# A weighted sum of two experts' outputs: the first small write of zeroes is taken out

## The chip, the core and the metric

The kernel runs on one core of one Trainium2 chip. The metric is the device time of one execution in microseconds; of three runs of the kernel before, the median is 238.86 us (238.84 to 238.99). The profile is of one execution, taken by the hardware profiler.

## The reference

Each of 16 x 1024 = 16,384 tokens has two vectors of 512 float32 numbers, one from each of its two experts, and two weights. The output is the weighted sum.

```python
# expert_outputs (16, 1024, 2, 512) f32, combine_weights (16, 1024, 2) f32
def reference(expert_outputs, combine_weights):
    weights = combine_weights[..., np.newaxis]
    return np.sum(expert_outputs * weights, axis=2).astype(np.float32)
```

The inputs are 67.2 MB (4 KB a token) and the output 33.6 MB (2 KB a token).

## The kernel before

The tokens are laid out over the 128 partitions: each partition holds 128 of them (`per`), the first 115 (`main`) from one contiguous stretch of the tokens and the last 13 (`LAST`) from another. A token's place in its partition is called `t`.

*Buffers.* One large tile, `et`, has room for 51 tokens a partition, cut into four rooms of 13, 13, 12 and 13 (`ROOM`). A tile of work is the 12 or 13 tokens a partition that fill one room; ten such tiles (`TILES`) make up the 128, and tile g uses room g mod 4. The output of a tile is written over its input, in the first half of a room, and stored from there. `wt` holds all the weights, 256 numbers a partition. `zt`, 16 x 128 numbers, holds zeroes, and `warm` is one column.

*Loads.* All loads of the expert outputs are issued by SP (L76). The first tile comes in two parts, of 2 and of 11 tokens a partition, so there are five loads ahead of the loop (`FIRST`): 1024, 5632, 6656, 6144 and 6656 KB. The first of them is cut into pieces of 4 KB. The other six are issued in the loop, each when the store out of its room is done.

*Small DMAs at the start.* ACT issues four, in this order: the zeroes (L111), the weights of the first 115 tokens a partition (L79, 920 bytes a partition), and the weights of the last 13 in two halves of 64 partitions (L114). Then it runs one activation on a constant (L115), which brings its table load with it. The zeroes are made by a memset on VectorE (L108). They go to the output itself: its first 115 x 128 rows are seen as 16 long rows, and the first 128 numbers of each (512 bytes) are written with zeroes. The tiles' results are stored over them later.

*The loop.* It runs over nine stores (`STORES`); tiles 7 and 8 share one. For tiles 0 to 7 `combine` multiplies a whole tile by its weights in one VectorE operation (L88) and adds the two halves in another (L97). Tile 8 shares its first product with ScalarE (L92, L94, L96, then L97). Tile 9 goes token by token: ScalarE scales one expert's vector (L102), and VectorE multiplies the other one and adds (L103). ACT issues the first seven stores and SP the last two (L130). SP then issues the load of the tile that takes the room's place (L76).

*Order.* The order of instructions on each queue is that of the program; the framework adds the waits. DMAs signal through a small set of semaphores used in turn, so a DMA also waits until the one that had its semaphore before it has landed.

Of the kernel before, what the change touches and what calls it, by code (L numbers as in the profile page):

```python
# [1 line left out]

# [4 lines left out]


@with_exitstack
def kernel(  # L10
    ctx: ExitStack,
    tc: tile.TileContext,
    expert_outputs: bass.AP,
    combine_weights: bass.AP,
    out: bass.AP,
):

    nc = tc.nc
    b, s, k, h = expert_outputs.shape
    assert k == 2
    n = b * s
    P = nc.NUM_PARTITIONS
    per = n // P
    assert per * P == n

    ROOM = [13, 13, 12, 13]
    ROOMS = len(ROOM)  # L30
    SITE = [sum(ROOM[:i]) for i in range(ROOMS)]
    TILES = [13, 13, 12, 13, 13, 13, 12, 13, 13, 13]
    FIRST = [2, 11, 13, 12, 13]
    STORES = [[0], [1], [2], [3], [4], [5], [6], [7, 8], [9]]
    WHOLE = [0, 1, 2, 3, 4, 5, 6, 7]
    MIXED = [8]
    ALONE = 3
    FREE = {9: 0}
    LAST = 13
    assert all(c <= ROOM[g % ROOMS] for g, c in enumerate(TILES))  # L40
    assert sum(TILES) == per and [g for st in STORES for g in st] == list(range(len(TILES)))
    main = per - LAST
    starts = [sum(TILES[:g]) for g in range(len(TILES))]

    def rows(x):

        first = x[0 : P * main, :].rearrange("(p t) f -> p t f", p=P)
        second = x[P * main : n, :].rearrange("(p t) f -> p t f", p=P)
        return lambda t, c: first[:, t : t + c, :] if t < main else second[:, t - main : t - main + c, :]

    flat = out.rearrange("b s h -> (b s) h")
    eo = rows(expert_outputs.rearrange("b s k h -> (b s) (k h)"))
    cw = rows(combine_weights.rearrange("b s k -> (b s) k"))
    o = rows(flat)

    dt = mybir.dt.float32
    mult = mybir.AluOpType.mult
    add = mybir.AluOpType.add
    copy = mybir.ActivationFunctionType.Copy

    pool = ctx.enter_context(tc.tile_pool(name="all", bufs=1))
    et = pool.tile([P, sum(ROOM), k * h], dt)
    halves = et.rearrange("p j (k h) -> p (j k) h", k=k)
    wt = pool.tile([P, per * k], dt)
    wk = wt.rearrange("p (t k) -> p t k", k=k)
    zt = pool.tile([16, 128], dt)
    warm = pool.tile([P, 1], dt)

    def place(t):
        g = max(g for g in range(len(TILES)) if starts[g] <= t)  # L70
        return SITE[g % ROOMS] + t - starts[g]

    def load(t, c, **kw):
        at = place(t)
        assert place(t + c - 1) == at + c - 1
        nc.sync.dma_start(out=et[:, at : at + c], in_=eo(t, c), **kw)  # L76

    def weights(q, t, c):
        q.dma_start(out=wk[:, t : t + c, :], in_=cw(t, c))  # L79

    def combine(g, base):
        at, c, t0 = SITE[g % ROOMS], TILES[g], starts[g]
        if g in WHOLE or g in MIXED:
            room = halves[:, k * at : k * (at + c), :]
            x0, x1 = et[:, at : at + c, 0:h], et[:, at : at + c, h : 2 * h]
            if g in WHOLE:
                wb = wt[:, k * t0 : k * (t0 + c)].unsqueeze(2).to_broadcast([P, k * c, h])
                nc.vector.tensor_tensor(out=room, in0=room, in1=wb, op=mult)  # L88
            else:
                for i in range(ALONE, c):  # L90
                    x = et[:, at + i, 0:h]
                    nc.scalar.activation(out=x, in_=x, func=copy, scale=wt[:, k * (t0 + i) : k * (t0 + i) + 1])  # L92
                w1 = wk[:, t0 : t0 + c, 1:2].to_broadcast([P, c, h])
                nc.vector.tensor_tensor(out=x1, in0=x1, in1=w1, op=mult)  # L94
                w0 = wk[:, t0 : t0 + ALONE, 0:1].to_broadcast([P, ALONE, h])
                nc.vector.tensor_tensor(out=x0[:, 0:ALONE], in0=x0[:, 0:ALONE], in1=w0, op=mult)  # L96
            nc.vector.tensor_tensor(out=halves[:, base : base + c, :], in0=x0, in1=x1, op=add)  # L97
            return
        for i in range(c):
            t = k * (t0 + i)  # L100
            x0, x1 = halves[:, k * (at + i), :], halves[:, k * (at + i) + 1, :]
            nc.scalar.activation(out=x0, in_=x0, func=copy, scale=wt[:, t : t + 1])  # L102
            nc.vector.scalar_tensor_tensor(  # L103
                out=halves[:, base + i, :], in0=x1, scalar=wt[:, t + 1 : t + 2], in1=x0, op0=mult, op1=add
            )

    with tc.manual_schedule():
        nc.vector.memset(zt, 0.0)  # L108

        ahead = flat[0 : P * main, :].rearrange("(q t) h -> q (t h)", q=16)  # L110
        nc.scalar.dma_start(out=ahead[:, 0:128], in_=zt)  # L111
        weights(nc.scalar, 0, main)
        for half in (slice(0, P // 2), slice(P // 2, P)):
            nc.scalar.dma_start(out=wk[half, main:per, :], in_=cw(main, per - main)[half])  # L114
        nc.scalar.activation(out=warm, in_=nc.const_aps.tensor(1.0, (P, 1), dt), func=copy)  # L115

        t = 0
        for i, c in enumerate(FIRST):
            load(t, c, **({"max_dma_last_dim": k * h * 4} if i == 0 else {}))
            t += c  # L120
        assert t == sum(TILES[:ROOMS])
        for j, st in enumerate(STORES):
            room = FREE.get(st[0], st[0] % ROOMS)
            base, c = SITE[room] * k, 0
            for g in st:
                combine(g, base + c)
                c += TILES[g]
            assert c <= k * ROOM[room]
            q = nc.sync if j in (7, 8) else nc.scalar
            q.dma_start(out=o(starts[st[0]], c), in_=halves[:, base : base + c, :])  # L130
            for g in st:
                if g + ROOMS < len(TILES):
                    load(starts[g + ROOMS], TILES[g + ROOMS])


# [1 line left out]
_INS = ['expert_outputs', 'combine_weights']  # L137
_OUTS = [((16, 1024, 512), 'float32')]


# [23 lines left out]
```

## Time and profile before

| | |
|---|---|
| median of three runs | 238.86 us |
| profiled execution, first to last instruction (span) | 237.1 us |
| VectorE busy | 190.0 us (80%), 33 instructions |
| ScalarE busy | 15.8 us (7%) |
| moved | 100.80 MB in 3344 packets, 425 GB/s over the span |
| queue q1 (issued by SP) | 2000 packets, 77.33 MB |
| queue q10 (issued by ACT) | 1344 packets, 23.47 MB |
| of the zeroes: memset, issue, issue to landing | 0.17 us, 0.39 us, 3.9 us |

The page gives no time of its own for the profiled execution beyond its span; the median of the runs stands 1.8 us above that span. In the profile, "issue" rows of SPq and ACTq are the time in which a sequencer issues a DMA, not the transfer; the time from issue to landing is listed apart, and contains the wait behind other transfers. The DMA row gives the mean busy share of the core's 16 DMA engines in tenths. A name such as out_dram<-zt reads "written from zt to the output".

### The profile page before, as it was taken

What the parts mean: (1) busy time and instruction counts of PE and PEld (TensorE: products, weight loads), DVE (VectorE), ACT (ScalarE), POOL (GpSimd) and SP (SyncE); (2) the same over time, 40 slices, a digit from 0 to 9 for tenths busy, and PEclk for the clock granted to TensorE, in tenths of its full rate; (3) what the DMA queues carried; (4) which work ended last, traced back from release to release, by engine and by line L of the source; (5) the groups of instructions that cost most, each with busy time, mean ns of one, the idle gap of its engine ahead of it and who ended that gap; (6) DMA issues with size and microseconds to landing.
All of it is one profiled execution on the core that took longest, in us unless ns stands there. A gap on an engine that the chain in (4) does not pass through costs nothing.

```text
span 237.1 us, 154 instructions
## 1 busy us (share of the span) xinstructions
DVE 190.0 (80%) x33; ACT 15.8 (7%) x25; POOL 0.2 (0%) x4
## 2 busy tenths in 40 slices
DVE  0006999999999999999999998998499969919400
ACT  2000000000000000000000000000000055019200
POOL 0000000000000000000000000000000000000000
DMA  8999999989999999999899999999899999899996
GB/s 300 388 481 434 432 421 398 470 348 485 449 431 458 431 440 390 486 420 420 359 492 409 409 509 392 431 503 431 359 431 503 420 397 483 381 431 431 431 431 287
DMA packets 3344, 100.80 MB, mean 425 GB/s; under 512 B 512, under 2 KB 656, under 8 KB 912
## 3 DMA queue, kind: packets, MB, share of 16 engines
q1 hardware_dynamic: 2000, 77.33, 75.9%
q10 hardware_dynamic: 1344, 23.47, 23.0%
HBM read 67.24 MB, written 33.56 MB: 425 GB/s over the span
## 4 chain that ended last, share of the span: by engine, by line
DVE 55%; DMA 36%; issue 1%; ACT 0%; DVEq 0%; ACTq 0%; SPq 0%
DVE et L88 35%; DVE et L97 17%; DMA out_dram<-et 17%; DMA et<-in_expert_outputs_dram 12%; DMA wt<-in_combine_weights_dram 8%; DVE et L103 3%; ACT et L102 0%; DVEq L159 0%; ACTq L111 0%; DVE zt L108 0%; DVEq L88 0%; SPq L76 0%; ACTq L102 0%
## 5 line engine op out<-in xcount | busy, mean ns | idle before, releaser
L88 DVE TENSOR_TENSOR et<-et,wt 128x13312 f32<-128x13312 f32 (+1 forms) x8 | 110.0, 13754 | 23.8 <-DMA wt<-in_combine_weights_dram 18.7
L97 DVE TENSOR_TENSOR et<-et 128x6656 f32<-128x6656 f32 (+1 forms) x9 | 62.8, 6973 | 0.4
L92 ACT ACTIVATE et<-et,wt 128x512 f32<-128x512 f32 x10 | 6.2, 708 | 188.0 <-DMA et<-in_expert_outputs_dram 188.0
L103 DVE SCALAR_TENSOR_TENSOR et<-et,wt 128x512 f32<-128x512 f32 x13 | 8.7, 747 | 5.0 <-ACT et L102 5.0
L102 ACT ACTIVATE et<-et,wt 128x512 f32<-128x512 f32 x13 | 8.1, 707 | 14.0 <-DMA et<-in_expert_outputs_dram 14.0
L94 DVE TENSOR_TENSOR et<-et,wt 128x6656 f32<-128x6656 f32 x1 | 7.1, 7093 | 2.3 <-DMA et<-in_expert_outputs_dram 2.3
L96 DVE TENSOR_TENSOR et<-et,wt 128x1536 f32<-128x1536 f32 x1 | 1.8, 1751 | 0.0
L115 ACT ACT_TABLE_LOAD x1 | 1.3, 1283 | 3.1 <-issue 3.1
L108 DVE MEMSET zt<- 16x128 f32 x1 | 0.2, 165 | 0.8 <-PEq L148 0.8
L115 ACT ACTIVATE warm<-const-float32-1.0 128x1 f32<-128x1 f32 x1 | 0.2, 203 | 0.0
L148 POOL MEMSET const-bfloat16-1.0<- 128x1 bf16 x1 | 0.1, 102 | 0.0
L148 POOL MEMSET const-uint8-127<- 128x1 uint8 x1 | 0.1, 101 | 0.0
L148 POOL MEMSET const-float32-0.0<- 128x1 f32 x1 | 0.1, 99 | 0.2 <-issue 0.2
L148 POOL MEMSET const-float32-1.0<- 128x1 f32 x1 | 0.1, 98 | 0.0
## 6 DMA issues: line engine op xcount, KB each, us to landing
et<-in_expert_outputs_dram SPq DMA_DIRECT2D x7, 6656.0 KB, 32.2
out_dram<-et ACTq DMA_DIRECT2D x5, 3328.0 KB, 34.7
et<-in_expert_outputs_dram SPq DMA_DIRECT2D x2, 6144.0 KB, 41.1
out_dram<-et SPq DMA_DIRECT2D x1, 6656.0 KB, 19.9
out_dram<-et ACTq DMA_DIRECT2D x2, 3072.0 KB, 37.2
et<-in_expert_outputs_dram SPq DMA_DIRECT2D x1, 5632.0 KB, 18.2
out_dram<-et SPq DMA_DIRECT2D x1, 3328.0 KB, 14.0
et<-in_expert_outputs_dram SPq DMA_DIRECT2D x1, 1024.0 KB, 5.0
```

The lines of the kernel that those rows point to most:

```text
L88: nc.vector.tensor_tensor(out=room, in0=room, in1=wb, op=mult)
L92: nc.scalar.activation(out=x, in_=x, func=copy, scale=wt[:, k * (t0 + i) : k * (t0 + i) + 1])
L94: nc.vector.tensor_tensor(out=x1, in0=x1, in1=w1, op=mult)
L96: nc.vector.tensor_tensor(out=x0[:, 0:ALONE], in0=x0[:, 0:ALONE], in1=w0, op=mult)
L97: nc.vector.tensor_tensor(out=halves[:, base : base + c, :], in0=x0, in1=x1, op=add)
L102: nc.scalar.activation(out=x0, in_=x0, func=copy, scale=wt[:, t : t + 1])
L103: nc.vector.scalar_tensor_tensor(out=halves[:, base + i, :], in0=x1, scalar=wt[:, t + 1 : t + 2], in1=x0, op0=mult, op1=add)
L108: nc.vector.memset(zt, 0.0)
L115: nc.scalar.activation(out=warm, in_=nc.const_aps.tensor(1.0, (P, 1), dt), func=copy)
L148: nc = _bacc.Bacc("TRN2", target_bir_lowering=False, num_devices=1)
```

## The change

The tile `zt`, its memset on VectorE and the DMA that writes it to 16 rows of the output are removed. Nothing else is edited. ACT's first DMA is then that of the weights.

```diff
     wk = wt.rearrange("p (t k) -> p t k", k=k)
-    zt = pool.tile([16, 128], dt)
     warm = pool.tile([P, 1], dt)
...
     with tc.manual_schedule():
-        nc.vector.memset(zt, 0.0)
-
-        ahead = flat[0 : P * main, :].rearrange("(q t) h -> q (t h)", q=16)
-        nc.scalar.dma_start(out=ahead[:, 0:128], in_=zt)
         weights(nc.scalar, 0, main)
         for half in (slice(0, P // 2), slice(P // 2, P)):
             nc.scalar.dma_start(out=wk[half, main:per, :], in_=cw(main, per - main)[half])
```

## The prediction

> **What bounds the kernel now.** I read the page first: its busy shares, the row of the DMA engines in forty slices, and the bytes.
>
> ```profile
> span 237.1 us, 154 instructions
> DVE 190.0 (80%) x33; ACT 15.8 (7%) x25; POOL 0.2 (0%) x4
> DMA  8999999989999999999899999999899999899996
> DMA packets 3344, 100.80 MB, mean 425 GB/s; under 512 B 512, under 2 KB 656, under 8 KB 912
> ```
>
> VectorE is busy for 80% of the span, but the row of the DMA engines reads 8 or 9 in every slice but the last. To see whether a transfer ever has to wait for an instruction, I took stretches of the windows view: the time before the first packet, the first load, two stretches in the middle, and the time behind the last packet. The columns are start:end, length, busy time of DVE, ACT and POOL, the clock, the share of the DMA engines and GB/s.
>
> ```profile
> 0.00:1.80 1.80, 0.17 (x1) 0.00 (x0) 0.20 (x4) 1.00 0.00 0
> 1.80:5.00 3.20, 0.00 (x0) 1.49 (x2) 0.00 (x0) 1.00 0.99 315
> 5.00:18.60 13.60, 0.00 (x0) 0.00 (x0) 0.00 (x0) 1.00 1.01 435
> 75.00:100.00 25.00, 24.97 (x3) 0.00 (x0) 0.00 (x0) 1.00 1.00 431
> 235.66:237.10 1.44, 0.00 (x0) 0.00 (x0) 0.00 (x0) 1.00 0.01 0
> ```
>
> The span is nearly a ledger of DMA work. 100.80 MB at 433 GB/s, the middle of 431 and 435, are 232.8 us; 1.80 us pass before the first packet and 1.44 us behind the last; that is 236.0 of 237.1 us. The rest, 1.1 us, is lost where the engines are occupied but slow. The first such place is visible above: in 1.80 to 5.00 they are 99% occupied and move 315 GB/s. At 433 GB/s the same bytes take 3.20 x 315/433 = 2.33 us, so 0.87 us go there. I looked for a second place around the first output store, whose issue the timeline gives (start, length). The three stretches below it are of the DMA view, 36.2 to 43.4, 43.4 to 46.1 and 46.1 to 51.0 us. Queue q1 carries what SP issues, the loads; q10 what ACT issues; the columns are packets, MB and share of 16 engines.
>
> ```profile
> 40.91 0.34 ACTq L130 DMA_DIRECT2D out_dram<-et  x1
> ...
> q1 hardware_dynamic: 64, 3.15, 101.0%
> ...
> q1 hardware_dynamic: 16, 0.79, 81.6%
> q10 hardware_dynamic: 16, 0.43, 36.6%
> ...
> q1 hardware_dynamic: 32, 1.57, 75.0%
> ```
>
> All these q1 packets belong to one load of the same 49,152 bytes a packet. Before the store's first packets one takes 1.010 x 7.2 x 16 / 64 = 1.82 us; just as they begin, 0.816 x 2.7 x 16 / 16 = 2.20 us; after that 0.750 x 4.9 x 16 / 32 = 1.84 us. So each engine loses about 0.38 us once, at the first store. 0.87 and 0.38 us are 1.25 us, which closes the ledger to within the 0.2 us that the choice of rate leaves open.
>
> Last, whether VectorE's waits could move the end. From the chain of waits (start, length, what):
>
> ```profile
> 1.43 18.21 DMA wt<-in_combine_weights_dram
> ...
> 19.73 14.04 DVE et L88
> ...
> 144.62 39.25 DMA out_dram<-et
> ...
> 183.92 28.80 DMA et<-in_expert_outputs_dram
> ```
>
> From 144.62 us the chain runs through transfers. Up to there VectorE is on it, but transfers are never out of work meanwhile (431 GB/s in 75 to 100 us). What a change does to the time is therefore what it does to the DMA engines: bytes taken away, and time lost in which they stand or crawl.
>
> **The change part by part.** What goes and what stands around it, from the timeline and from the table of issues (KB, us from issue to landing):
>
> ```profile
> 0.73 0.44 SPq L76 DMA_DIRECT2D et<-in_expert_outputs_dram  x1
> 0.81 0.17 DVE L108 MEMSET zt<- 16x128 f32 x1 [0.81 <-PEq L148]
> 1.01 0.39 ACTq L111 DMA_DIRECT2D out_dram<-zt  x1
> 1.22 0.46 SPq L76 DMA_DIRECT2D et<-in_expert_outputs_dram  x1
> 1.43 0.45 ACTq L79 DMA_DIRECT2D wt<-in_combine_weights_dram  x1
> 1.91 1.16 ACTq L114 DMA_DIRECT2D wt<-in_combine_weights_dram  x2
> et<-in_expert_outputs_dram SPq DMA_DIRECT2D x1, 5632.0 KB, 18.2
> et<-in_expert_outputs_dram SPq DMA_DIRECT2D x1, 1024.0 KB, 5.0
> wt<-in_combine_weights_dram ACTq DMA_DIRECT2D x1, 115.0 KB, 18.2
> out_dram<-zt ACTq DMA_DIRECT2D x1, 8.0 KB, 3.9
> ```
>
> *The memset, 0.17 us*, is alone on VectorE, which has nothing to do before 19.73 us: nothing on the path. If VectorE started at once it would cost 0.17 us.
>
> *The zeros' packets.* In 4.0 to 4.6 us the DMA view has them, 16 packets of data and 16 that signal:
>
> ```profile
> q1 hardware_dynamic: 59, 0.24, 97.7%
> q10 hardware_dynamic: 32, 0.01, 6.0%
> ```
>
> 0.060 x 0.6 us = 0.036 us of each engine. By the ledger this is gained whole: -0.04 us.
>
> Against this row stands a rule. The Trainium skill, page "DMA: Bandwidth & Descriptors", section "Rules for kernel authors", says that a transfer under 64 KB is mostly overhead. By it the 3.9 us to landing of this 8 KB transfer would be nearly all overhead to be saved; the trace does not agree that it is on the path, since the loads kept 97.7% of the engines meanwhile.
>
> *The weights move up.* ACT waits for the memset until 1.01 us and issues the weights at 1.43. Without both it can issue them as soon as SP issues its first load, at 0.73 us, 0.70 us sooner, and the two tail DMAs behind them likewise. In 8 to 10 us the queues alternate, one packet of the weights (920 bytes) for one of the load of 5632 KB on each engine:
>
> ```profile
> q1 hardware_dynamic: 16, 0.72, 83.2%
> q10 hardware_dynamic: 16, 0.01, 2.1%
> ```
>
> So eight packets of weights took eight load packets of 0.832 x 2 = 1.66 us to get through, and landed at 1.43 + 18.21 = 19.64 us. If they come up among the small packets of the first load, they land before the 5632 KB load does, and then that load is next to be late: issued at 1.22, landed at 19.4 us. VectorE starts 0.2 to 0.3 us sooner. By the ledger this is worth nothing at the end; without the cover of saturated engines it would be worth those 0.3 us.
>
> *The two sequencers meet.* The issue that all else waits for, SP's first at 0.73, now meets ACT's long one in place of the zeros' at 1.01. An issue of SP beside one of ACT takes up to 0.64 us (least, median and most of the four in ns stand in the second row), one that is alone 0.33:
>
> ```profile
> 2.20 0.64 SPq L76 DMA_DIRECT2D et<-in_expert_outputs_dram  x1
> L76 SPq DMA_DIRECT2D et<-in_expert_outputs_dram x4: 424/449/643, 0.7 to 2.2; - x4
> 67.80 0.33 SPq L76 DMA_DIRECT2D et<-in_expert_outputs_dram  x1
> ```
>
> The first takes 0.44 now. At worst the weights' issue goes wholly ahead of it, +0.45 us; at best nothing. I take 0.64 - 0.44 = +0.20 us, since every delay before the first packet is added to the span. The Trainium skill, page "Perfetto Trace Analysis", section "DMA Instruction — HWDGE (DVE, Sync)", says that two sequencers share one block that generates descriptors; the longer issues agree, and no row here shows which comes first.
>
> *The first write.* The zeros are the first bytes that the kernel writes to the output, one small packet on each of 16 engines, at a time when a write can be held up without holding up the loads. Two first uses are seen to cost the engines time: 0.87 us at the first load, 0.38 us at the first store, and the second of these with the zeros long landed. If a first write has a cost of its own, the zeros paid it hidden, and the store at 40.91 us now pays it with full engines. The trace cannot show it. From below, it is zero: the zeros landed 3.9 us after issue with no dent in the loads. From above, it is the 0.87 us of the first load. A gain is excluded by the loads' 97.7% in those 0.6 us. I take the nearest row, the same event with large packets: +0.38 us, a stall that doubles.
>
> *The fifth load.* SP's queue shows one wait on the zeros:
>
> ```profile
> SPq L76 <- DMA out_dram<-zt: 2.1, 1, 2.1
> 4.92 0.33 SPq L76 DMA_DIRECT2D et<-in_expert_outputs_dram  x1
> et<-in_expert_outputs_dram SPq DMA_DIRECT2D x1, 6656.0 KB, 71.7
> et<-in_expert_outputs_dram SPq DMA_DIRECT2D x1, 6144.0 KB, 50.9
> ```
>
> The fifth load shares a semaphore with the zeros and is held until they have landed. It is issued at 4.92 us and lands 71.7 us later, behind the fourth load, which is issued at 2.20 and lands at 2.20 + 50.9 = 53.1 us. So it stood in the queue for some 48 us. Whether another DMA holds it next or none, its place in the queue is the same: 0. It would matter only if it were held until shortly before 53 us.
>
> Sum: -0.04 + 0.20 + 0.38 = +0.54 us. The profiled span of 237.1 becomes 237.6 us; the median of the runs, 238.86, stands 1.8 us above the span, outside the instructions, which the change leaves alone. So 238.86 + 0.54 = 239.4 us, 0.23% slower.
>
> **The rivals.**
>
> *Work is conserved, no change.* The two plus terms are zero; -0.04 us gives 238.8 us. For it: the ledger, and zeros that landed without a dent in the loads. Against it: both stalls that the ledger needs sit at a first use. Chance 0.36, and 0.02 more for a change that only moves the fifth load's wait.
>
> *Faster: a cleaner start.* The slow 3.2 us hold the issue of the zeros and of three weight DMAs among the first loads' issues. If the crowd of issues is what starves the first load, one issue fewer and the weights out of the way sooner give back part of the 0.87 us. At half, 0.44 + 0.04 = 0.48 us: 238.4 us. It decides from the point at which the start window's rate passes 365 GB/s (0.44 us less for the same bytes). Against it: packets are slowest at the very beginning, while the zeros' packets pass at full rate. Chance 0.13.
>
> *Faster by the whole wait.* If the fifth load's 2.1 us in SP's queue came through to the end: 238.86 - 2.1 = 236.8 us. That needs the queue of loads to run dry, and the load stood in it for some 48 us. It is also what the overhead rule above would make of the time. Chance 0.02.
>
> **How the numbers follow.** The forecast's case, a slower start or a slower first store, has 0.47. A measurement of this kernel can tell about 0.2%, 0.48 us, from no change; so the forecast lies just past that bound, with its own range from 238.9 to 240.2 (+0.45 and +0.87, less 0.04). The cases give faster 0.15, same 0.38, slower 0.47. The range over all reaches down to 238.3, which takes in the conserved case and the cleaner start at a little over half, and up to 240.2.
>
> **What would show it.** In the changed profile: ACT's first issue near 0.7 us and SP's first issue longer than 0.44; the first packet later than 1.8 us; the weights landing before the 5632 KB load, and VectorE starting near 19.5; above all the packets of the fourth load, 1.82 us each, stretching to more than 2.2 us when the first store begins. If they stretch as before and the first packet comes at 1.8, the conserved case is right and I am wrong. If the rate in the first 3.2 us of packets rises past 365 GB/s, it is the cleaner start.

## The result and the profile after

The changed kernel takes 239.69 us, the median of six runs, against 238.89 us for the kernel before: a ratio of 1.0026 with a 95% interval of 1.0016 to 1.0036. That is slower by 0.8 us in the medians, and inside the forecast range (239.4, 238.3 to 240.2).

The six runs are not one cluster. Five lie between 239.53 and 239.74 us and one at 238.85, where the kernel before stands. The profile after is of that one. A second profile, of a run at 239.55 us, is that of the run "same_again" below. I call the two the short and the long execution of the changed kernel. Of eleven runs in both series one is short.

The page of the short execution has the span and the busy times of the kernel before:

```profile
span 237.1 us, 151 instructions
DVE 189.9 (80%) x32; ACT 15.8 (7%) x25; POOL 0.2 (0%) x4
```

The long one spans 237.8 us. The timelines of both begin with the same two issues, short first, then long. ACT's weights and SP's first load are issued within 0.01 us of each other, where the kernel before had 0.28 us between SP's load and ACT's zeroes:

```profile
0.72 0.43 ACTq L78 DMA_DIRECT2D wt<-in_combine_weights_dram  x1
0.73 0.44 SPq L75 DMA_DIRECT2D et<-in_expert_outputs_dram  x1
...
0.72 0.45 ACTq L78 DMA_DIRECT2D wt<-in_combine_weights_dram  x1
0.73 0.42 SPq L75 DMA_DIRECT2D et<-in_expert_outputs_dram  x1
```

Where the long execution loses its 0.7 us is seen in four stretches of the windows view, in this order: the start, the first store, the whole middle, the tail. First the kernel before (its start stands in the prediction), then the long execution:

```profile
41.00:52.00 11.00, 11.00 (x1) 0.00 (x0) 0.00 (x0) 1.00 0.97 402
52.00:212.00 160.00, 148.90 (x17) 6.23 (x10) 0.00 (x0) 1.00 1.00 433
235.40:237.00 1.60, 0.00 (x0) 0.00 (x0) 0.00 (x0) 1.00 0.01 0
...
1.80:5.00 3.20, 0.00 (x0) 1.49 (x2) 0.00 (x0) 1.00 0.98 315
41.00:52.00 11.00, 11.00 (x2) 0.00 (x0) 0.00 (x0) 1.00 0.98 383
52.00:212.00 160.00, 149.26 (x17) 6.23 (x10) 0.00 (x0) 1.00 1.00 434
235.40:237.00 1.60, 0.00 (x0) 0.00 (x0) 0.00 (x0) 1.00 0.16 67
```

The start moves 315 GB/s in both and the 160 us of the middle 433 and 434. The 11 us around the first store drop from 402 to 383 GB/s, which is 11 x 19/402 = 0.52 us. Behind 235.4 us the kernel before has no data left to begin, the long execution has 67 GB/s x 1.6 us = 0.11 MB, four packets of 26,624 bytes. This tail is mostly the loss of the first store coming out at the end, and not a second loss to be added to it. The DMA view of 234.6 to 235.0 us before, and of 235.0 to 235.6 us in the long execution, has each time the last packet of all 16 engines (columns: packets, MB, share of 16 engines):

```profile
q1 hardware_dynamic: 16, 0.43, 246.8%
...
q1 hardware_dynamic: 16, 0.43, 164.5%
```

So every engine ends later, and the sixteen last packets begin within 0.6 us of each other in place of 0.4. A loss of some 0.5 us on every engine, and the wider spread, which the last engine sets, make the 0.7 us. In the short execution both stretches are as before:

```profile
41.00:52.00 11.00, 11.00 (x1) 0.00 (x0) 0.00 (x0) 1.00 0.98 402
235.40:237.00 1.60, 0.00 (x0) 0.00 (x0) 0.00 (x0) 1.00 0.01 0
```

The engines are out of step long before the end. The DMA view of 18.95 to 20 us shows it at the start of the third load (53,248 bytes a packet). In the kernel before no packet starts there, all 16 engines have moved on. In the long execution eight packets do, of 0.21 MB together, which is the third load's first packet on four engines and four packets that signal. The short execution, second row, has one engine there:

```profile
q1 hardware_dynamic: 8, 0.21, 47.0%
...
q1 hardware_dynamic: 2, 0.05, 11.8%
```

The two executions differ already in whose packets come first, though ACT's issue is 0.01 us ahead in both. In 1.8 to 2.2 us the short one moves ACT's packets (q10) and a single one of SP's load (q1); the long one, last row, moves SP's alone:

```profile
q10 hardware_dynamic: 39, 0.04, 82.6%
q1 hardware_dynamic: 1, 0.00, 2.5%
...
q1 hardware_dynamic: 18, 0.07, 160.2%
```

In the next 1.6 us the long execution has 78 of ACT's packets among 88 of the load's. In the kernel before ACT's first packets come behind 3.8 us.

At the first store the engines' step decides which of them takes the store's packet when. The next rows are of 45.4 to 46.4 and of 46.4 to 48.4 us, the kernel before first, the long execution second:

```profile
q10 hardware_dynamic: 16, 0.43, 98.7%
q1 hardware_dynamic: 16, 0.79, 92.5%
...
q10 hardware_dynamic: 13, 0.35, 80.2%
q1 hardware_dynamic: 2, 0.10, 30.4%
q1 hardware_dynamic: 14, 0.69, 99.9%
q10 hardware_dynamic: 1, 0.03, 3.1%
```

Before, all 16 engines take the store's first packet in the same microsecond, and the load packets behind it take 0.925 x 2 x 16 / 16 = 1.85 us. In the long execution 13 take it; others go on with a load packet first and come to the store 2 us later; and the load packets of the next round take 0.999 x 2 x 16 / 14 = 2.28 us. The round ahead of the store is slow in both: here is 43.4 to 44.0 us before, 3.671 x 0.6 x 16 / 16 = 2.20 us a packet, and 43.2 to 44.1 us in the long execution, 2.591 x 0.9 x 16 / 16 = 2.33 us:

```profile
q1 hardware_dynamic: 16, 0.79, 367.1%
...
q1 hardware_dynamic: 16, 0.79, 259.1%
```

So the stall at the first store, one slow round before, takes two rounds in the long execution.

### The profile page after: what moved, and what is told of

Same layout as the page of the kernel before. It is cut to its first block, busy times and chain, and to the rows that moved or that the text cites. A ratio compares the mean times of both kernels' runs of the same rounds, so it can differ in the third digit from the quotient of the medians.

```text
span 237.1 us, 151 instructions
## 1 busy us (share of the span) xinstructions
DVE 189.9 (80%) x32; ACT 15.8 (7%) x25; POOL 0.2 (0%) x4
## 3 DMA queue, kind: packets, MB, share of 16 engines
q10 hardware_dynamic: 1312, 23.46, 23.2%
## 4 chain that ended last, share of the span: by engine, by line
DVE 53%; DMA 36%; issue 3%; ACT 0%; DVEq 0%; SPq 0%; ACTq 0%
DVE et L87 35%; DMA et<-in_expert_outputs_dram 20%; DMA out_dram<-et 17%; DVE et L96 15%; DVE et L102 3%; ACT et L101 0%; DVEq L154 0%; SPq L75 0%; DVEq L87 0%; ACTq L101 0%
```

## The experiments

Each run is timed against the kernel before on its own chip. Diffs are against the changed kernel unless said otherwise.

**same_again.** No edit.

> The changed kernel itself, once more, with another profile. Both theories expect what was seen: most runs 0.7 to 0.9 us above the kernel before (span near 237.9 us), few at its time (span 237.1 us). If the profile is of a long run, theory M (the two sequencers meet: ACT's weights and SP's first load are issued within some 10 ns of each other) expects the first load's start or its slow stretch to be 0.5 to 0.9 us worse than in the profile of 237.1 us, and the packets around the first store as there (2.2 us). Theory W (the first write costs time) expects the start unchanged and the fourth load's packets around the first store to take 2.6 us or more instead of 2.2.

Measured: 239.76 us, ratio 1.0037 (1.0025 to 1.0049), five of five runs long. The profile is the long one above: the loss is at the first store, where theory W looked, but as two rounds of 2.3 us and not one of 2.6; the 315 GB/s of the start, where theory M looked, are unchanged, but the engines leave it out of step. So each theory has half.

**memset_only.**

```diff
+        nc.vector.memset(wt[0:16, 0:128], 0.0)
         weights(nc.scalar, 0, main)
```

> The changed kernel with a memset of a corner of the weights' tile ahead of the weights' DMA, so that ACT issues the weights at about 1.0 us, after SP's first issue has begun, and nothing is written to the output early. Theory M: 238.9 us in every run, span 237.1. Theory W: as the changed kernel, 239.7 us in most runs.

Measured: 238.97 us, ratio 1.0008 (0.9990 to 1.0026). With ACT's issue at 1.01 us and no early write the loss is gone but for 0.1 us, in eleven of twelve runs. Its profile, of a run at 239.17 us, has 402 GB/s around the first store.

```profile
0.73 0.42 SPq L75 DMA_DIRECT2D et<-in_expert_outputs_dram  x1
0.81 0.17 DVE L107 MEMSET wt<- 16x128 f32 x1 [0.81 <-PEq L144]
1.01 0.38 ACTq L78 DMA_DIRECT2D wt<-in_combine_weights_dram  x1
```

**zeros_last.** The kernel before with its memset and zeroes' DMA moved behind the weight DMAs (the tile `zt` is back).

```diff
             nc.scalar.dma_start(out=wk[half, main:per, :], in_=cw(main, per - main)[half])
+        nc.vector.memset(zt, 0.0)
+        ahead = flat[0 : P * main, :].rearrange("(q t) h -> q (t h)", q=16)
+        nc.scalar.dma_start(out=ahead[:, 0:128], in_=zt)
```

> The zeroes are written as in the kernel before, but behind ACT's three weight DMAs, so that ACT's first issue is that of the weights, beside SP's first. Theory M: as the changed kernel, 239.7 us in most runs. Theory W: 238.9 us, since the first write is still paid early.

Measured: 239.65 us, ratio 1.0033 (1.0021 to 1.0045), all five runs 239.53 to 239.81. The zeroes land 23.2 us after their issue at 2.41 us, well before the first store at 41.3 us, and nothing is gained: theory W, the first write, falls. The same windows as above show the same two signs, weaker than in same_again:

```profile
41.00:52.00 11.00, 11.00 (x2) 0.00 (x0) 0.00 (x0) 1.00 0.99 392
235.40:237.00 1.60, 0.00 (x0) 0.00 (x0) 0.00 (x0) 1.00 0.08 33
```

**small_read_first.** ACT reads 16 pieces of the inputs into `zt`, which is kept, ahead of the weights.

```diff
+        few = expert_outputs.rearrange("b s k h -> (b s) (k h)").rearrange("(q t) f -> q (t f)", q=16)
+        nc.scalar.dma_start(out=zt, in_=few[:, 0:128])
         weights(nc.scalar, 0, main)
```

> In place of the zeroes' write ACT reads 16 pieces of 512 bytes of the expert outputs into the same buffer, at once, with no memset: a small DMA meets SP's first issue at 0.72 us, the weights follow at about 1.2, and nothing is written early. Theory M: what meets SP's first load is now 16 packets and not 128, so between 238.9 us (if the number of packets makes the loss) and 239.7 (if the meeting itself does). Theory W: 239.7 us in most runs.

Measured: 239.90 us, ratio 1.0040 (1.0027 to 1.0053). Sixteen small packets do as much harm as 128, so it is the meeting of the issues and not the number of packets. The profile is of the longest run, 240.32 us. Eight engines begin the third load behind 18.95 us (first row, 18.95 to 20 us), and the loss sits in the tail: engines out of step, with hardly a second stall.

```profile
q1 hardware_dynamic: 16, 0.43, 94.3%
41.00:52.00 11.00, 11.00 (x2) 0.00 (x0) 0.00 (x0) 1.00 0.96 399
235.40:237.00 1.60, 0.00 (x0) 0.00 (x0) 0.00 (x0) 1.00 0.20 83
```

**warm_first.** ACT's warming activation moved ahead of its DMAs.

```diff
+        nc.scalar.activation(out=warm, in_=nc.const_aps.tensor(1.0, (P, 1), dt), func=copy)
         weights(nc.scalar, 0, main)
...
-        nc.scalar.activation(out=warm, in_=nc.const_aps.tensor(1.0, (P, 1), dt), func=copy)
```

> The changed kernel with ACT's table load and warming activation put ahead of its weight DMAs, which are then issued near 2.2 us, when SP's first four loads have been issued. Theory M (what costs the time is that ACT's first issue meets SP's first): 238.9 us in every run, the 16 engines in step as in the kernel before. The weights land after the 5632 KB load, near 20 to 22 us, so VectorE starts up to 2 us later; by the ledger of DMA work this costs nothing. A rival, VectorE's start is on the path: 240 us or more.

Measured: 239.67 us, ratio 1.0031 (1.0014 to 1.0048). The edit did not do what it was for: ACT issued its DMA beside its own table load, 0.06 us behind SP.

```profile
0.72 1.28 ACT L107 ACT_TABLE_LOAD   x1 [0.72 <-PEq L143]
0.72 2.15 SPq L75 DMA_DIRECT2D et<-in_expert_outputs_dram  x4
0.78 0.40 ACTq L78 DMA_DIRECT2D wt<-in_combine_weights_dram  x1
```

So it is one more meeting, with SP first this time, and as costly. Whether VectorE's start matters was not tested here.

**sp_waits.**

```diff
+        nc.vector.memset(et[0:16, 0:1, 0:128], 0.0)
         weights(nc.scalar, 0, main)
```

> The changed kernel with a memset of a corner of the first room ahead of SP's first load, so that SP issues it near 1.0 us, after ACT's weights at 0.72 us. All transfers of the loads start 0.28 us later. Theory M, in which only the meeting hurts: 238.86 + 0.28 = 239.1 to 239.2 us in every run, the engines in step. Rival, weights ahead of or among the first load's packets hurt by themselves: 239.7 us or more.

Measured: 239.95 us, ratio 1.0040 (1.0012 to 1.0068), in two groups: six runs of 238.91 to 239.05 and six of 240.86 to 241.05. The profile is of a run at 239.05: 402 GB/s around the first store, nothing behind 235.4 us. In these six the time is even below the 239.1 of theory M. The other half is explained by neither theory. Three of the 82 runs of the kernel before that were timed beside the experiments also took 240.5 to 241.2 us, and one of the twelve of memset_only 241.1; there is no profile of such a run.

**weights_on_sp.** The weights' DMA is issued by SP behind the first load, the two tails by SP behind the fourth.

```diff
             t += c
+            if i == 0:
+                weights(nc.sync, 0, main)
+            if i == 3:
+                for half in (slice(0, P // 2), slice(P // 2, P)):
+                    nc.sync.dma_start(out=wk[half, main:per, :], in_=cw(main, per - main)[half])
```

> The changed kernel with the weights' DMA issued by SP behind its first load, and the two tails by SP behind its fourth: ACT issues nothing before the first store, so nothing meets. Theory M: 238.8 to 238.9 us in every run, the weights landing near 7 us. Rival (the first load's slow start has nothing to do with ACT's issues, and the zeroes or the memset protect by something else): 239.7 us.

Measured: 240.51 us, ratio 1.0059 (1.0038 to 1.0079), scattered from 239.6 to 241.3. A miss for theory M, and the profile (of a run at 239.63 us) shows another loss. Around the first store it has 402 GB/s, but 60 to 66 us, where the second store begins, fall from 426 in the kernel before to 382:

```profile
60.00:66.00 6.00, 6.00 (x2) 0.00 (x0) 0.00 (x0) 1.00 0.98 426
...
60.00:66.00 6.00, 6.00 (x2) 0.00 (x0) 0.00 (x0) 1.00 0.92 382
```

The tails' small packets stood in SP's queue among the loads, the first store passed them and landed 18.2 us after its issue, against 26.8 before; so ACT's queue was empty when the second store came, and that one stalled too. That reading is from one profile and was not tested by itself; nor does it say what makes these runs scatter.

**four_engines_late** and **three_late.** Both start from the kernel before, zeroes and all, and were meant to put some engines behind. The first (upper lines) copies 24 KB to each of four rows of the output that are stored over later, the second (lower lines) loads 16 KB to each of three partitions:

```diff
+        few = expert_outputs.rearrange("b s k h -> (b s) (k h)")[0:24, :].rearrange("(q t) f -> q (t f)", q=4)
+        nc.scalar.dma_start(out=flat[0:48, :].rearrange("(q t) h -> q (t h)", q=4), in_=few)
...
             t += c
+            if i == 0:
+                nc.sync.dma_start(out=et[0:3, SITE[3] : SITE[3] + 4], in_=eo(0, 4)[0:3])
```

> The kernel before, zeroes and all, with one more DMA by ACT behind the weights: four pieces of 24 KB copied from the inputs to rows of the output that are stored over later, one piece on each of four DMA engines, so that these four fall about 0.9 us behind the other twelve before the first store. Theory S (a lag of single engines is never made up, and the first store stalls longer when the engines are out of step): at least 238.9 + 0.9 = 239.8 us, up to 240.4, and a second round of stretched load packets at the first store. Rival (the engines share the work out again): the mean lag of 0.2 us, 239.1 us.

> The kernel before, zeroes and all, with one more DMA by SP behind its first load: three pieces of 16 KB of the inputs, one for each of three partitions, into the corner of a room that the fifth load fills later. If the pieces stay on three DMA engines, these fall 16,384 / 27.1 = 0.60 us behind the other 13 at the start of the second load, as far as in the long runs of the changed kernel, while ACT's issues meet SP's no more than before. Theory S (engines out of step make the first store stall twice): three or so engines take their first store packet one load packet late (after 48 us), a second round of the fourth load's packets is stretched to 2.2 us or more, the other engines too end 0.4 to 0.5 us late, and the time is 239.5 to 240.0 us. Rival (being out of step is only a mark of something else): one round of stretched packets as before, 13 engines end on time and only three 0.6 us late, 239.4 us; or, if the pieces are split over all engines, 0.11 us, 239.0 us.

The first came out at 239.09 us against 238.86, +0.23 (ratio 0.9997, 0.9975 to 1.0019, an interval widened by two runs of the kernel before above 241). It does not test theory S: the profile has 33 packets more under 8 KB than the kernel before (945 against 912), too many for four pieces, so the copy was split over all engines. It agrees with the ledger: 98 KB over 16 engines are 6,144 bytes each, at 433/16 = 27.1 GB/s 0.23 us, and the median grew by 0.23 us.

The second put engines behind, and cost more than was expected: 240.39 us, ratio 1.0063 (1.0049 to 1.0076), five runs within 0.2 us. Now only three engines take the store's first packet at 45.4 to 46.4 us and 13 do so in the next two:

```profile
q1 hardware_dynamic: 5, 0.25, 73.6%
q10 hardware_dynamic: 3, 0.08, 18.5%
q1 hardware_dynamic: 6, 0.29, 44.2%
q10 hardware_dynamic: 13, 0.35, 40.1%
```

Behind 235.4 us there are 100 GB/s x 1.6 us = 0.16 MB, the last packet of six engines, though only three were put behind. So a lag of single engines is not made up, and it costs the others time as well; with ACT's first issues just as in the kernel before. The sizes were off: 1.5 us where theory S had 0.6 to 1.1, and the engines split 3 and 13, not 13 and 3. And the second stall that theory S expects is not there: 41 to 52 us move 401 GB/s, against 402 before, and one round of load packets is slow, that of 44.7 to 47.1 us with 0.988 x 2.4 x 16 / 16 = 2.37 us a packet (first row below). VectorE's first product also starts 1.2 us later than before (20.96 us), and so does ACT's first store, so the two profiles differ in more than the engines' step.

```profile
q1 hardware_dynamic: 16, 0.79, 98.8%
41.00:52.00 11.00, 11.00 (x2) 0.00 (x0) 0.00 (x0) 1.00 0.99 401
235.40:237.00 1.60, 0.00 (x0) 0.00 (x0) 0.00 (x0) 1.00 0.24 100
```

**weights_late.**

```diff
+        for _ in range(3):
+            nc.vector.memset(wt[:, 0 : k * main], 0.0)
         weights(nc.scalar, 0, main)
```

> The changed kernel with three memsets of the weights' tile ahead of the weights' DMA, so that ACT's first issue comes near 1.7 us, well behind SP's first (0.73 to 1.17 us). Theory M (the loss is made where ACT's first issue meets SP's first, which puts the 16 engines out of step): 238.8 to 238.9 us in every run, the engines at the start of the second load no more than 0.4 us apart; the weights land at 20 us or later and VectorE starts up to 1 us late, which costs nothing. Rival (ACT must issue something small early, as the zeroes were): 239.7 us.

Measured: 238.91 us, ratio 1.0004 (0.9995 to 1.0012); ten of eleven runs lie between 238.85 and 239.00, one is at 239.40. No zeroes, no DMA by ACT before 1.85 us, and the whole loss is gone. VectorE did not start later, as was expected, but at 19.55 us. The timeline and the first store (45.4 to 46.4 and 46.4 to 48.4 us) of its profile:

```profile
0.84 0.98 DVE L108 MEMSET wt<- 128x230 f32 x3 [0.84 <-PEq L145]
1.85 0.38 ACTq L78 DMA_DIRECT2D wt<-in_combine_weights_dram  x1
...
q10 hardware_dynamic: 16, 0.43, 98.7%
q1 hardware_dynamic: 16, 0.79, 91.0%
```

All 16 engines take the store together, as in the kernel before.

**write_soon** and **write_both.** A second theory of the stall itself: that ACT's queue has been idle for too long. In the changed kernel and in the kernel before, zeroes are written near 34 us.

```diff
                 nc.vector.tensor_tensor(out=room, in0=room, in1=wb, op=mult)
+                if g == 0:
+                    nc.vector.memset(zs, 0.0)
+                    soon = flat[0 : P * main, :].rearrange("(q t) h -> q (t h)", q=16)
+                    nc.scalar.dma_start(out=soon[:, 0:128], in_=zs)
```

> The changed kernel with the zeroes' write moved to the moment when VectorE has multiplied the first tile, near 34 us, some 7 us ahead of the first store; ACT's weights still meet SP's first load. Theory Q (the first store stalls the engines because ACT's queue has been idle for some 20 us): the fourth load's packets at the first store take 2.2 us or less, and the time falls from 239.7 to 239.2 or below. Theory S (they stall because the engines come to it out of step): still 239.6 to 239.8 us.

> The kernel before, with its zeroes at the start, and a second write of zeroes near 34 us as in the run above. Theory Q: the stall of 0.38 us at the first store goes, 238.5 us. Theory S: 238.9 us, the engines being in step already.

Measured: write_soon 240.13 us, ratio 1.0046 (1.0034 to 1.0059), with 378 GB/s in 41 to 52 us (its profile is of a run at 239.66 us), so the stall is there in full; write_both 239.14 us, 1.0011 (1.0002 to 1.0020), with 402. In write_both the first store is issued at 42.17 us, when the zeroes have landed, and a slow round comes with it all the same: 45.0 to 46.5 us, 1.526 x 1.5 x 16 / 16 = 2.29 us a packet (16 packets, 152.6% of 16 engines). Theory Q falls: a write some 7 us ahead takes nothing off the stall. Why a first store stalls the engines at all stays open.

## Why the prediction was right, and where it was not

The direction, the size and the place held: 239.69 us against 239.4, and the fourth load's packets at the first store stretch where the prediction told the reader to look. The reasons given for both plus terms were wrong, so that their sum came within 0.3 us is in part luck. (The upper end of the range, +0.45 and +0.87 less 0.04, comes to 240.1 us, not 240.2.)

- *The zeroes' packets, -0.04 us*: too small to be seen; four_engines_late agrees with the ledger that it rests on (0.23 us of added work by the bytes, 0.23 us in the medians). The rule of the Trainium skill on small transfers, page "DMA: Bandwidth & Descriptors", section "Rules for kernel authors", does not help here: taking out an 8 KB transfer saved nothing that can be measured.
- *The two sequencers meet, +0.20 us*: the trigger is right, the way is not. I priced a longer first issue of SP and a later start. SP's first issue takes 0.42 us in the long execution, not 0.64, its load's first packets begin by 1.8 us, and the start moves 315 GB/s as before; the price is paid by engines that leave the start out of step. In the short execution the load's packets do come later, only one of them before 2.2 us, and nothing is lost. Kernels in which ACT's first issue is within 0.06 us of SP's (same_again, zeros_last, small_read_first, warm_first, write_soon) take 239.65 to 240.13 us; kernels in which it comes 0.28 us (memset_only) or 1.1 us (weights_late) behind take 238.97 and 238.91. In the profiles of the first five, four to eight engines begin the third load behind 18.95 us; in those of memset_only, weights_late and the faster run of sp_waits none does. The Trainium skill, page "Perfetto Trace Analysis", section "DMA Instruction — HWDGE (DVE, Sync)", says that two sequencers share the block that makes descriptors; a loss that is there with two issues within 0.06 us of each other and gone with 0.28 us between them agrees with it. What happens inside that block no run shows.
- *The first write, +0.38 us*: the step that failed. I took the cover of the zeroes to be that they paid for the first write. zeros_last still has that early write and loses; weights_late has none and does not. In place of this term the long execution loses 0.52 us more at the first store, most of it in a second slow round, on engines that are already out of step, and has a wider spread at the end. What makes the second round is not shown: small_read_first and three_late have engines out of step and 399 and 401 GB/s there.
- *The weights move up, 0*: they landed 4.6 us after issue in the long execution, not 18.2. VectorE did not start 0.2 to 0.3 us sooner, though: in the long execution its first product starts at 20.00 us, behind the late engines' part of the second load. In every profile of the first five kernels named above it starts at 20.00 us or later, against 19.41 to 19.73 us in the kernel before, memset_only, weights_late and the faster run of sp_waits; no run separates the late start from the engines' step. That the late start costs nothing of its own is argued from the engines, which are fully occupied and move 434 GB/s through the 160 us of the middle.
- *The memset and the fifth load, 0*: nothing in the profiles speaks against them.
- *The rivals*: no change came true in one run of eleven, 238.85 us. A cleaner start did not come (315 GB/s in the long execution, 330 in the short one, where 365 were asked for), and the 2.1 us of the fifth load's wait were not on the path.

In other words the zeroes are a spacer. What they kept apart was ACT's first issue and SP's; a memset that ACT must wait for does the same. That engines out of step end late is supported by three_late, which put them out of step by other means; that they make the second stall is not. Why a meeting leaves the engines in step in one run of eleven was not tested. The profiles point to the order of the packets: in the one short execution, and in the faster run of sp_waits, ACT's packets come ahead of SP's first load, in the five long profiles behind its first packets and among them. Open as well are the runs near 241 us in sp_waits and the scatter of weights_on_sp, which loses time though ACT issues nothing at the start. No version beat the kernel before; weights_late equals it.

## What to carry to other kernels

In a kernel whose DMA engines never rest, ask of a small step at the start not only what it costs but what it keeps apart in time: its wait may be worth more than its work. A lag that single DMA engines took on early was still there at the end here, so look for packets of the last transfer that begin after most engines are done. And if runs of one kernel fall into two groups, profile one of each before explaining the median.

## What was not expected of the hardware

Two DMA issues from different sequencers, 0.01 us apart, cost 0.7 to 0.8 us more than the same two 0.28 us apart (medians of 239.69 and 239.76 against 238.97 us), in ten runs of eleven. A copy of four rows of 24 KB between two places in HBM was spread over more engines than four (33 packets more), while a load of three rows of 16 KB to three partitions was not (q1 has 2006 packets against 2000: three of data and three that signal). And an ACT DMA written behind an activation in the program was issued 0.06 us after the activation's table load began, not after it ended.
